# Last projection of an encoder layer: activation sums on VectorE, a written order for the stage, a fourth raw buffer, and the low parts of one product by an accumulating DMA

## The chip, the core and the metric

The kernel runs on one core of a Trainium2 chip. TensorE (PE) multiplies, VectorE (DVE), ScalarE (ACT) and GpSimd (POOL) work elementwise, SyncE (SP) issues most DMAs and GpSimd the others. Every engine takes its instructions in the order in which they stand in the program, and waits on semaphores. Time is device time of one execution in microseconds (us); lower is better.

## The reference

One transformer-like layer on 512 tokens of width 1024, in fp32: a mixer, a cross-attention, a gated feed-forward block, and a last norm. The change touches the end of it alone: the product with `w_down`, the residual sum and the norm.

```python
def swiglu(h, w_gate, w_up, w_down):
    return (jax.nn.silu(h @ w_gate) * (h @ w_up)) @ w_down
...
        x = x + swiglu(rms_norm(x, norm_ffn_g[l]), w_gate_ffn[l], w_up_ffn[l], w_down_ffn[l])
    return rms_norm(x, final_g)
```

The hidden width is 2816, so `w_down` is 2816 x 1024 and the activations are 512 x 2816.

## The kernel before

**How a product is made.** An fp32 factor is cut in two: ScalarE copies it to a rounded high part (`hi`, tiles `wh`, `arh`, `aTh`), VectorE subtracts that from the source to get the low part (`lo`, tiles `wl`, `arl`, `aTl`). Three matmuls (hi x hi, hi x lo, lo x hi) stand for one. `split` does both halves of the cut, and `part` issues the six matmuls (two rows of 128 hidden columns times three) of one token tile with one cut piece of weights.

**The stage.** The hidden columns lie in eleven pairs of 128. Three pairs (`NP = 3`, `c` = 0, 1, 2) are multiplied plainly by `plain` into both column halves of the output. The other eight (`NS = 8`, tile `afb`) go through a scheme of seven block products in place of eight: `a11`, `a12`, `a21`, `a22` are the blocks by parity of the hidden tile and by half of the tokens, `W` is cut alike. Three products take their activations as they lie and four take sums of blocks, formed in place in `afb`; four take differences of weights, two of them formed in place in `wx` (which holds the raw block that several differences need). A product has four chunks of weights (each 128 x 1024 fp32, a half of a raw tile `wr`) and, for each, two token tiles, so eight calls of `part`, 48 matmuls 512 columns wide. The results collect in the PSUM tiles `pa`, `pb`, `pc`, `pd` (`pd` is the second pair of the tiles named `pb` in the trace) and `pe` (named `pf` there); `into` adds a result to the residual `xr` on VectorE, `done` and `last_norm` finish a token tile, and the outputs are stored as they become ready.

**Who did the sums.** `asum` forms the four sums of activations in two halves each, eight instructions on GpSimd (L1212). `wsub` forms the differences of weights on VectorE (L1227). `left` cuts the activations, `prod` the weights (both through `split`, L104 on ScalarE and L105 on VectorE).

**What set the order.** The stage before it (class `Seven`, the gate and up projections) is pinned: instructions recorded with `pin` keep the order in which they are written. The last projection's instructions were not pinned, apart from a few in `fill`: a scheduler placed each of them by its own estimate, between and behind pinned ones. Raw weights go through three buffers (tag `wr`), cut weights through six (tag `wh`/`wl`, `WB = 6`), cut activations through five.

```python
    def asum(o, p, q, op):
        for hs_ in AH:
            nc.gpsimd.tensor_tensor(out=o[:, hs_], in0=p[:, hs_], in1=q[:, hs_], op=op)
```

Of the kernel before, what the change touches and what calls it, by code (L numbers as in the profile page):

```python
# [17 lines left out]
def encoder_kernel(  # L18
# [82 lines left out]
    def split(src, hi, lo, scale=None):

        if scale is None:
            nc.scalar.copy(out=hi, in_=src)  # L104
            nc.vector.tensor_tensor(out=lo, in0=src, in1=hi, op=ALU.subtract)  # L105
# [1057 lines left out]
    def part(dst, a, w, first, last):  # L1163

        n = 0
        for u, v in ((0, 0), (0, 1), (1, 0)):
            for k in range(2):
                nc.tensor.matmul(dst, a[u][:, k, :], w[v][:, k, :], start=first and n == 0, stop=last and n == 5,  # L1168
                                 skip_group_check=True)
# [40 lines left out]
    def asum(o, p, q, op):  # L1210
        for hs_ in AH:
            nc.gpsimd.tensor_tensor(out=o[:, hs_], in0=p[:, hs_], in1=q[:, hs_], op=op)  # L1212
# [5 lines left out]
    def wload(par, half, h, dst=None):  # L1218
        if dst is None:
            return load_raw(wsrc(par, half, h), NS // 2, 512)  # L1220
        nc.sync.dma_start(out=dst, in_=wsrc(par, half, h))
        return dst

    PAIRS = [slice(2 * j, 2 * j + 2) for j in range(NS // 4)]

    def wsub(o, p, q):
        nc.vector.tensor_tensor(out=o, in0=p, in1=q, op=ALU.subtract)  # L1227
        return o

    def wraw(par, half, dst=None):  # L1230

        for h in range(2):
            r = wload(par, half, h, dst and dst[:, AH[h]])
            for sl in PAIRS:
                yield r[:, sl]

    def wform(par, half, f):

        for h in range(2):
            r = wload(par, half, h)  # L1240
            for sl in PAIRS:
                yield f(r[:, sl], wx[:, AH[h]][:, sl])

    def prod(dsts, a, ws, first, last, tail=0):

        pcs = []
        n = NS // 2
        for c, src in enumerate(ws):
            h = wp.tile([P, 2, 512], F32R, name=nm("wh"), tag="wh", bufs=WB)
            l = wp.tile([P, 2, 512], F32R, name=nm("wl"), tag="wl", bufs=WB)  # L1250
            split(src, h, l)
            pcs.append((h, l))

        def go(c, t):
            k = 2 * c % (NS // 2)
            part(dsts[t], [v[:, k:k + 2, TOK[t]] for v in a[2 * c // (NS // 2)]], pcs[c],
                 first and c == 0, last and c == n - 1)

        for c in range(n - tail):
            for t in range(2):  # L1260
                go(c, t)
        for t in range(2):
            for c in range(n - tail, n):
                go(c, t)
# [10 lines left out]
    a11, a12, a21, a22 = blk(0, 0), blk(1, 0), blk(0, 1), blk(1, 1)
    open_a(2)
    for t in range(2, NT):
        plain(bd.dsts[t], 0, 1, t)
    asum(a21, a21, a22, ALU.add)
    l12 = left(a12)  # L1280
    for t in range(NT):
        plain(bd.dsts[t], 0, 2, t)
    open_a(0)
    close(apa)
    ep = pool("ep")
    gfin = ep.tile([P, D], F32, name="gfin")
    nc.gpsimd.dma_start(out=gfin, in_=final_g.partition_broadcast(P))

    xg = {}

    def last_norm(t, half):
        rs = square_half(ep, t, xr[t], half, lead[t])
        if half == lead[t]:
            if t == NT - 1:
                xg[t] = ep.tile([P, 512], F32, name="xg")
                nc.vector.tensor_tensor(out=xg[t], in0=xr[t][:, HALVES[half]], in1=gfin[:, HALVES[half]], op=ALU.mult)
            return
        o = ep.tile([P, D], F32, name=nm("o"), tag="o", bufs=2)
        for h in (lead[t], 1 - lead[t]):
            cs = HALVES[h]  # L1300
            if h == lead[t] and t in xg:
                nc.scalar.activation(out=o[:, cs], in_=xg[t], func=AF.Copy, scale=rs)
            else:
                nc.vector.scalar_tensor_tensor(out=o[:, cs], in0=xr[t][:, cs], scalar=rs, in1=gfin[:, cs],
                                               op0=ALU.mult, op1=ALU.mult)
            nc.sync.dma_start(out=out[t * P:(t + 1) * P, cs], in_=o[:, cs])
# [7 lines left out]
    prod(pb, l12, wraw(1, 0), False, True)  # L1314
    into(pb, 0, 0)
    l11 = left(a11)
    prod(pa, l11, wraw(0, 0, wx), True, True)
    into(pa, 0, 0)
    done(0, 0)
    asum(a11, a21, a11, ALU.subtract)  # L1320
    s1 = left(a21)
    asum(a12, a12, a11, ALU.subtract)
    prod(pc, s1, wform(0, 1, lambda w, x_: wsub(x_, w, x_)), True, True)
    into(pc, 1, 1)
    asum(a21, a22, a11, ALU.subtract)
    s2 = left(a11)
    prod(pa, s2, wform(1, 1, lambda w, x_: wsub(x_, w, x_)), False, True)
    into(pa, 0, 1)
    pe = [acc() for t in range(2)]
    for c in range(NP):  # L1330
        for t in range(NT):
            dst = pc[t] if t < 2 else pe[t - 2]
            plain(dst, 1, c, t, first=t >= 2 and c == 0, last=c == NP - 1)
    into(pe, 1, 1)
    s4 = left(a12)
    prod(pc, s4, wraw(1, 1), False, True)
    into(pc, 0, 1)
    done(0, 1)
    s3 = left(a21)
    prod(pa, s3, wform(0, 0, lambda w, x_: wsub(w, x_, w)), False, True)  # L1340
    into(pa, 1, 1)
    done(1, 1)
    into(pa, 1, 0)
    l22 = left(a22)
    prod(pd, l22, wform(1, 0, lambda w, x_: wsub(w, w, x_)), False, True, tail=2)
    for t in range(2):
        nc.vector.tensor_tensor(out=xr[2 + t][:, HALVES[0]], in0=pd[t], in1=xr[2 + t][:, HALVES[0]], op=ALU.add)
# [41 lines left out]
```

## Time and profile before

| | us |
|---|---|
| median of 3 runs | 970.9 (970.65 to 973.08) |
| the profiled execution | 969.74 |
| its span, first to last instruction | 968.0 |
| PE busy | 945.1 |
| DVE busy | 705.4 |
| ACT busy | 480.1 |
| POOL busy | 259.1 |
| granted TensorE clock, mean | 0.992 |

Every line of the profile belongs to the one profiled execution. A row of the timeline has the start, the duration, the engine, the source line (L1168 is line 1168), the operation, tiles written and read, and how many instructions were merged into the row; a bracket at its end is the idle time before it and what ended that. The last projection begins at about 841.7 us, with the first matmul of `part`.

### The profile page before, as it was taken

What the parts mean: (1) busy time and instruction counts of PE and PEld (TensorE: products, weight loads), DVE (VectorE), ACT (ScalarE), POOL (GpSimd) and SP (SyncE); (2) the same over time, 40 slices, a digit from 0 to 9 for tenths busy, and PEclk for the clock granted to TensorE, in tenths of its full rate; (3) what the DMA queues carried; (4) which work ended last, traced back from release to release, by engine and by line L of the source; (5) the groups of instructions that cost most, each with busy time, mean ns of one, the idle gap of its engine ahead of it and who ended that gap; (6) DMA issues with size and microseconds to landing.
All of it is one profiled execution on the core that took longest, in us unless ns stands there. A gap on an engine that the chain in (4) does not pass through costs nothing. (4 is left out here: it accounts for less than half of the span.)

```text
span 968.0 us, 14495 instructions
## 1 busy us (share of the span) xinstructions
PE 945.1 (98%) x5894; PEld 849.1 (88%) x5894; DVE 705.4 (73%) x859; ACT 480.1 (50%) x742; POOL 259.1 (27%) x215
## 2 busy tenths in 40 slices
PE   7999999999999999999999999999999999998996
PEld 7988888888999999988988887899999999987785
DVE  6677887668965667566835445699888888799975
ACT  6474665435544545437635334554555455553632
POOL 1221122263411544321000000144454544264000
PEclk8999999999999999999999999999999999999998
DMA  8421221320432333381553211204333324452532
GB/s 292 144 88 44 87 78 54 120 88 22 131 109 88 110 89 109 101 290 44 175 173 131 87 44 49 79 5 131 99 120 102 118 88 130 153 196 87 177 106 87
DMA packets 83682, 107.12 MB, mean 111 GB/s; under 512 B 2096, under 2 KB 63584, under 8 KB 83616
## 3 DMA queue, kind: packets, MB, share of 16 engines
q1 hardware_dynamic: 82368, 101.74, 32.2%
q0 software_dynamic: 1248, 4.46, 1.3%
q8 instruction: 46, 0.75, 0.3%
q14 instruction: 20, 0.16, 0.1%
HBM read 104.10 MB, written 2.10 MB: 110 GB/s over the span
## 5 line engine op out<-in xcount | busy, mean ns | idle before, releaser
L105 DVE TENSOR_TENSOR wl<-wr,wh 128x1024 fp32r<-128x1024 f32 x100 | 124.9, 1259 | 63.0 <-ACT wh L104 37.3
L272 DVE TENSOR_TENSOR wl<-wr,wh 128x1024 fp32r<-128x1024 f32 x93 | 136.1, 1474 | 29.2 <-ACT wh L267 29.2
L104 ACT CAST wh<-wr 128x1024 fp32r<-128x1024 f32 x100 | 103.6, 1049 | 88.6 <-PE pq L142 20.9
L267 ACT CAST wh<-wr 128x1024 fp32r<-128x1024 f32 x93 | 97.7, 1052 | 26.1 <-DVE wr L257 26.1
L174 POOL TENSOR_TENSOR rs<-ve,mhalf 128x1 f32<-128x1 f32 x22 | 14.5, 661 | 314.6 <-DVE ve L172 249.7
L250 POOL TENSOR_TENSOR s<-wr 128x512 f32<-128x512 f32 x31 | 40.7, 1313 | 114.6 <-DVE w L272 110.4
L286 ACT COPY u<-pf 128x256 f32<-128x256 f32 x62 | 23.2, 374 | 93.2 <-DVE g L1098 33.8
L251 POOL TENSOR_TENSOR wr<-wr 128x512 f32<-128x512 f32 x31 | 64.6, 2084 | 2.4
L806 POOL TENSOR_TENSOR merged<-merged,sg 128x512 f32<-128x512 f32 x16 | 27.5, 1724 | 79.9 <-DVE sg L805 79.9
L582 POOL TENSOR_SCALAR_AFFINE_SELECT ab<-ab 128x128 f32<-128x128 f32 x32 | 23.8, 776 | 80.1 <-ACT ab L579 80.1
L280 PE MATMUL pf<-h3th,wh 128*128 128x256 f32 x240 | 37.1, 277 | 0.4 <-ACT m L286 0.4
L280 PE MATMUL pf<-h3tl,wh 128*128 128x256 f32 x240 | 37.0, 276 | 0.0
L280 PE MATMUL pf<-h3th,wl 128*128 128x256 f32 x240 | 37.0, 276 | 0.0
L286 ACT COPY m<-pf 128x256 f32<-128x256 f32 x31 | 11.6, 373 | 47.3 <-PE pf L280 45.1
L280 PEld LDWEIGHTS pf<-h3th,wh 128*128 128x128 f32 x240 | 31.7, 188 | 0.7 <-ACT m L286 0.6
L280 PEld LDWEIGHTS pf<-h3tl,wh 128*128 128x128 f32 x240 | 31.7, 188 | 0.0
L280 PEld LDWEIGHTS pf<-h3th,wl 128*128 128x128 f32 x240 | 31.7, 188 | 0.0
L257 DVE TENSOR_TENSOR wr<-wr 128x512 f32<-128x512 f32 x31 | 30.2, 975 | 1.1
L183 ACT ACTIVATE jk<-xr 128x512 f32<-128x512 f32 x24 | 15.1, 630 | 30.5 <-DVE xr L886 13.1
L1125 POOL TENSOR_TENSOR afb<-afb,g 128x256 f32<-128x256 f32 (+1 forms) x16 | 19.4, 1210 | 36.9 <-DVE afb L1098 36.9
L1212 POOL TENSOR_TENSOR afb<-afb 128x1024 f32<-128x1024 f32 x8 | 27.1, 3403 | 7.6 <-DVE arl L105 7.5
L280 PE MATMUL pf<-h3h,wh 128*128 128x256 f32 x160 | 25.6, 282 | 2.1 <-DVE g L1098 2.1
(381 smaller groups left out, 2638.3 us busy)
## 6 DMA issues: line engine op xcount, KB each, us to landing
wr<-in_w_in_dram SPq DMA_DIRECT2D x26, 1024.0 KB, 5.3
wr<-in_w_down_ffn_dram SPq DMA_DIRECT2D x14, 1024.0 KB, 5.1
wr<-in_w_gate_ffn_dram SPq DMA_DIRECT2D x11, 1024.0 KB, 5.4
wr<-in_w_up_ffn_dram SPq DMA_DIRECT2D x11, 1024.0 KB, 5.4
wb<-in_w_branch_dram SPq DMA_DIRECT2D x12, 512.0 KB, 3.3
wr<-in_w_out_dram SPq DMA_DIRECT2D x4, 1024.0 KB, 8.9
wr<-in_w_k_xa_dram SPq DMA_DIRECT2D x4, 1024.0 KB, 8.7
wr<-in_w_v_xa_dram SPq DMA_DIRECT2D x4, 1024.0 KB, 5.1
```

The source lines that it names most:

```text
L104: nc.scalar.copy(out=hi, in_=src)
L105: nc.vector.tensor_tensor(out=lo, in0=src, in1=hi, op=ALU.subtract)
L250: pin(nc.gpsimd.tensor_tensor(out=self.s1, in0=r[:, 0:4, P:256], in1=r[:, 4:8, P:256], op=ALU.add))
L251: pin(nc.gpsimd.tensor_tensor(out=r[:, 0:4, P:256], in0=r[:, 0:4, 0:P], in1=r[:, 0:4, P:256], op=ALU.subtract))
L257: pin(nc.vector.tensor_tensor(out=r[:, 4:8, 0:P], in0=r[:, 4:8, 0:P], in1=r[:, 0:4, 0:P], op=ALU.subtract))
L267: pin(nc.scalar.copy(out=t[0], in_=src))
L272: pin(nc.vector.tensor_tensor(out=l, in0=src, in1=h, op=ALU.subtract))
L280: pin(nc.tensor.matmul(dst[:, 0:256], w[:, k, :], v[:, k, :], start=first and n == 0, stop=last and n == 11, skip_group_check=True))
L286: pin(nc.scalar.copy(out=m, in_=self.a[:, 0:256]))
L582: nc.gpsimd.affine_select(out=dg, in_=dg, compare_op=ALU.is_gt, fill=0.0, base=0, channel_multiplier=1, pattern=[[-1, P]])
L806: pin(nc.gpsimd.tensor_tensor(out=merged[:, d, :], in0=merged[:, d, :], in1=sg, op=ALU.add))
L1212: nc.gpsimd.tensor_tensor(out=o[:, hs_], in0=p[:, hs_], in1=q[:, hs_], op=op)
```

## The change

Four things are changed, all in the last projection:

1. The eight sums of activations go from GpSimd to VectorE (`dsub`, L1207). GpSimd keeps the four small powers of the last norm and DMA issues.
2. All of the stage is pinned in a written order. The work is a list of steps, one per chunk of weights (two token tiles, 12 matmuls). Around the matmuls of step i - 5 the list issues the cut of step i, the sums and differences of step i + 2, and the loads of step i + 4; a low part is issued on VectorE one step behind its high part. The plain products of column half 1 are split: two pairs stand between the third product and the fourth, the last pair behind the fifth product. The norm's first squares of token tiles 0 and 1 move from behind the second product to behind the fourth.
3. A fourth buffer for raw weights: every fourth raw tile lies in a pool of its own.
4. In the third product (into `pc`, sum `a21 + a22`) the four low parts of the weights are made without VectorE: ScalarE writes minus the high part into `wl` (L1201), and a DMA issued by GpSimd adds the source to it (L1202). Source and destination are both in SBUF, 512 KB each.

The two cut tiles of plain pair 2 and of pair 0 lie in tiles of their own, and cut activations have four buffers instead of five. The order of the matmuls within a chunk, and the split of the last product by token tile (`tail=2`), stay.

```diff
-                nc.tensor.matmul(dst, a[u][:, k, :], w[v][:, k, :], start=first and n == 0, stop=last and n == 5,
-                                 skip_group_check=True)
+                pin(nc.tensor.matmul(dst, a[u][:, k, :], w[v][:, k, :], start=first and n == 0, stop=last and n == 5,
+                                     skip_group_check=True))
...
-    def asum(o, p, q, op):
-        for hs_ in AH:
-            nc.gpsimd.tensor_tensor(out=o[:, hs_], in0=p[:, hs_], in1=q[:, hs_], op=op)
+    los = []
+
+    def cut_pinned(src, hi, lo, added=False):
+        pin(nc.scalar.copy(out=hi, in_=src))
+        if added:
+            pin(nc.scalar.activation(out=lo, in_=hi, func=AF.Copy, scale=-1.0))
+            pin(nc.gpsimd.dma_start(out=lo, in_=src, accum_op=ALU.add))
+        else:
+            los.append(lambda: dsub(lo, src, hi))
+
+    def dsub(o, p, q, op=ALU.subtract):
+        pin(nc.vector.tensor_tensor(out=o, in0=p, in1=q, op=op))
...
+    RAWS = 4
+    raws = {"n": 0}
+
+    def raw_tile():
+        raws["n"] += 1
+        if raws["n"] % RAWS == 0:
+            return ad1.tile([P, NH, 512], F32, name=nm("wr"), tag="wr", bufs=1)
+        return wp.tile([P, NH, 512], F32, name=nm("wr"), tag="wr", bufs=3)
...
+        def sums(c):
+            h = c // 2
+            if c % 2 == 0 and asum is not None:
+                dsub(act[:, AH[h]], *(v[:, AH[h]] for v in asum[:2]), *asum[2:])
+            sl = slice(2 * (c % 2), 2 * (c % 2) + 2)
+            x_ = wx[:, AH[h]][:, sl]
+            src[c] = x_ if wraw is None else got[h][:, sl]
+            if wform is not None:
+                src[c] = wform(src[c], x_)
...
+    product(PB, a12, None, (1, 0), None, False, lambda: into(pb, 0, 0))
+    product(PA, a11, None, None, None, True, lambda: into(pa, 0, 0))
+    product(PC, a21, (a21, a22, ALU.add), (0, 1), tform(True, False), True, lambda: into(pc, 1, 1), added=True)
+    for q in zip(half1(0), half1(1)):
+        for v in q:
+            step(*v)
+    product(PA, a11, (a21, a11), (1, 1), tform(True, False), False, after6)
+    product(PC, a12, (a12, a11), (1, 1), None, False, lambda: None)
+    q = half1(2)
+    step(*q[0])
+    step(*q[1], post=lambda: (after3(), into(hold["e"], 1, 1)))
+    product(PA, a21, (a22, a11), (0, 0), tform(False, True), False, after7)
+    product(PD, a22, None, (1, 0), tform(False, False), False, after4, tail=2)
+
+    HIS, SUM, MORE = 5, 2, 4
+    late = {}
+    for i in range(-MORE, len(steps) + HIS):
+        for k, d in ((0, MORE), (1, SUM), (2, 0)):
+            if 0 <= i + d < len(steps):
+                steps[i + d][k]()
+        late[i], los[:] = los[:], []
+        for f in late.pop(i - 1, ()):
+            f()
+        if i >= HIS:
+            steps[i - HIS][3]()
+            steps[i - HIS][4]()
```

The order of instructions on the engines shows what moves. GpSimd, in the fourth-last pair of the gate and up projections (L1125 is the product of gate and up, L250 and L251 are sums of gate or up weights):

```order
 L1125 TENSOR_TENSOR afb<-afb,g_7411 128x256
 L1125 TENSOR_TENSOR afb<-afb,g_7411 128x512
-L1212 TENSOR_TENSOR afb<-afb 128x4x256
 L250 TENSOR_TENSOR s_7689<-wr_7550 128x512
 L251 TENSOR_TENSOR wr_7550<-wr_7550 128x4x128
```

One half of a sum of activations had been placed there, well ahead of the last projection; it is gone. GpSimd, from the last product of gate and up to the end:

```order
 L1125 TENSOR_TENSOR afb<-afb,g_8389 128x256
 L1125 TENSOR_TENSOR afb<-afb,g_8389 128x512
-L1212 TENSOR_TENSOR afb<-afb 128x4x256
-L1287 DMA gfin<-in_final_g_dram 128x1024
-L1212 TENSOR_TENSOR afb<-afb 128x4x256 x6
...
+L1202 DMA wl_8751<-wx 128x1024
+L1202 DMA wl_8774<-wx 128x1024
+L1202 DMA wl_8795<-wx 128x1024
+L1202 DMA wl_8812<-wx 128x1024
+L1360 DMA gfin<-in_final_g_dram 128x1024
```

The seven other halves are gone too; four accumulating DMAs stand in their place, and the load of the last gain `gfin` now follows them. VectorE after the change, from the adds of the first product's result (`pb`, L1241) through the differences and cuts that the second and third product need (`wx` rows are differences of weights, `afb` rows sums of activations):

```order
L1241 TENSOR_TENSOR xr_3935<-pb_8509,xr_3935 128x512
L1241 TENSOR_TENSOR xr_3936<-pb_8510,xr_3936 128x512
L1207 TENSOR_TENSOR wx<-wr_8664,wx 128x1024
L1207 TENSOR_TENSOR arl_8707<-afb,arh_8706 128x1024
L1207 TENSOR_TENSOR wl_8710<-wx,wh_8709 128x1024
L1207 TENSOR_TENSOR afb<-afb 128x4x256
L1207 TENSOR_TENSOR wx<-wr_8702,wx 128x1024
L1207 TENSOR_TENSOR wl_8727<-wx,wh_8726 128x1024
L1207 TENSOR_TENSOR wx<-wr_8702,wx 128x1024
L1207 TENSOR_TENSOR arl_8748<-afb,arh_8747 128x1024
```

And VectorE before, at the same place:

```order
L1227 TENSOR_TENSOR wx<-wr_8829,wx 128x1024
L105 TENSOR_TENSOR arl_8824<-afb,arh_8823 128x1024
L1227 TENSOR_TENSOR wx<-wr_8829,wx 128x1024
L105 TENSOR_TENSOR wl_8758<-wx,wh_8757 128x1024
L1227 TENSOR_TENSOR wx<-wr_8841,wx 128x1024
L1269 TENSOR_TENSOR xr_3935<-pb_8509,xr_3935 128x512
L105 TENSOR_TENSOR wl_8833<-wx,wh_8832 128x1024
L1269 TENSOR_TENSOR xr_3936<-pb_8510,xr_3936 128x512
```

Before, the adds of `pb` stood among the differences for the third product, four `wl` rows of which follow; now they stand ahead of these, the sums stand among them, and the third product has no `wl` row here. The end of VectorE's row, before (L1347 adds the last product, L188 and L172 make the norm's factor, L1304 writes the output `o`):

```order
L1347 TENSOR_TENSOR xr_3937<-pb_8511,xr_3937 128x512
L188 TENSOR_TENSOR st_9361<-ss_9268,ss_9359 128x1
L172 TENSOR_SCALAR ve_9363<-st_9361 128x1
L1304 SCALAR_TENSOR_TENSOR o_9367<-xr_3937,rs_9365,gfin 128x512 x2
L1347 TENSOR_TENSOR xr_3938<-pb_8512,xr_3938 128x512
L188 TENSOR_TENSOR st_9376<-ss_9271,ss_9374 128x1
```

And after:

```order
L1402 TENSOR_TENSOR xr_3937<-pb_8511,xr_3937 128x512
L188 TENSOR_TENSOR st_9355<-ss_9306,ss_9353 128x1
L172 TENSOR_SCALAR ve_9357<-st_9355 128x1
L1402 TENSOR_TENSOR xr_3938<-pb_8512,xr_3938 128x512
L1377 SCALAR_TENSOR_TENSOR o_9361<-xr_3937,rs_9359,gfin 128x512 x2
L188 TENSOR_TENSOR st_9382<-ss_9309,ss_9380 128x1
```

The add of the last token tile has moved ahead of the two output instructions of the tile before it.

More of the change, by code (lines that the diff above doesn't have):

```diff
@@ L1216, in wsrc, with wload, step, ring @@
         return w[:, AH[h]]
[L1218 to L1264, printed above, removed]
+    RAWS = 4
[5 more added lines that the diff above has]
+        return wp.tile([P, NH, 512], F32, name=nm("wr"), tag="wr", bufs=3)
+    def wload(par, half, h):
+        r = raw_tile()
+        pin(nc.sync.dma_start(out=r, in_=wsrc(par, half, h)))
+        return r
+    steps = []
+    def step(prep, mul, post=lambda: None, load=lambda: None, sums=lambda: None):
+        steps.append((load, sums, prep, mul, post))
+    def ring(src, added=False):
+        h = wp.tile([P, 2, 512], F32R, name=nm("wh"), tag="wh", bufs=WB)
+        l = wp.tile([P, 2, 512], F32R, name=nm("wl"), tag="wl", bufs=WB)
+        cut_pinned(src, h, l, added)
+        return h, l
     def into(dsts, i, half):
@@ L1273, in done @@
             last["f"](2 * i + t, half)
[L1275 to L1306, printed above, removed]
@@ L1308, in encoder_kernel, with product, load, prep @@
-    lead = (0, 0, 1, 1)
-    last["f"] = last_norm
+    def product(dsts, act, asum, wraw, wform, first, post, added=False, tail=0):
+        got, arr = {}, {}
+        def load(c):
+            if c % 2 == 0 and wraw is not None:
+                got[c // 2] = wload(*wraw, c // 2)
+        src = {}
+        def sums(c):
[7 more added lines that the diff above has]
+                src[c] = wform(src[c], x_)
+        def prep(c):
+            for h in range(2):
+                if c == (0 if tail else 2 * h):
+                    arr[h] = tuple(ad1.tile([P, NH, T // 2], F32R, name=nm(f"ar{s}"), tag=f"ar{s}", bufs=4)
+                                   for s in "hl")
+                    cut_pinned(act[:, AH[h]], *arr[h])
+            arr["w", c] = ring(src[c], added)
+        def go(c, t):
+            k = 2 * (c % 2)
+            part(dsts()[t], [v[:, k:k + 2, TOK[t]] for v in arr[c // 2]], arr["w", c], first and c == 0, c == 3)
+        def mul(c):
+            if c < 4 - tail:
+                for t in range(2):
+                    go(c, t)
+            elif c == 3:
+                for t in range(2):
+                    for k in range(4 - tail, 4):
+                        go(k, t)
+                    if t == 0:
+                        post(0)
+        if asum is None and wraw == (1, 0) and not tail:
+            load0, load = load, lambda c: (load0(c), c == 0 and load_x())
+        for c in range(4):
+            step(lambda c=c: prep(c), lambda c=c: mul(c),
+                 (lambda: post(1) if tail else post()) if c == 3 else lambda: None, lambda c=c: load(c),
+                 lambda c=c: sums(c))
@@ L1310, in encoder_kernel @@
+    step(cut2, lambda: plain0(0, (2, 3)))
+    step(prep2, lambda: plain0(1, (2, 3)))
+    step(lambda: None, lambda: plain0(2, (0, 1)))
+    step(lambda: None, lambda: plain0(2, (2, 3)))
     pa = [bank(nm("pa")) for t in range(2)]
@@ L1312, in encoder_kernel @@
     pb, pd = bd.dsts[:2], bd.dsts[2:]
[L1314 to L1343, printed above, removed]
@@ new lines, in encoder_kernel, with after6, after3, after7 @@
+    lead = (0, 0, 1, 1)
+    def after6():
+        into(pa, 0, 1)
+        last["ep"] = open_ep()
+        done(0, 0)
+    def after3():
+        into(pc, 0, 1)
+    def after7():
+        into(pa, 1, 1)
+        done(0, 1)
+        done(1, 1)
+        into(pa, 1, 0)
+    def after4(t):
+        o = xr[2 + t][:, HALVES[0]]
+        nc.vector.tensor_tensor(out=o, in0=pd[t], in1=o, op=ALU.add)
+        last["f"](2 + t, 0)
+    product(PB, a12, None, (1, 0), None, False, lambda: into(pb, 0, 0))
+    product(PA, a11, None, None, None, True, lambda: into(pa, 0, 0))
```

88 lines of the change are left out of this document (70 added, 18 removed).

## The prediction

> **What bounds the kernel now.** I read the page's head first, then TensorE's waits, then the busy time of the last projection's stretches, then its timeline around each wait.
>
> ```profile
> span 968.0 us, 14495 instructions
> PE 945.1 (98%) x5894; PEld 849.1 (88%) x5894; DVE 705.4 (73%) x859; ACT 480.1 (50%) x742; POOL 259.1 (27%) x215
> ...
> PE pa L1168 <- DVE wl L105: 3.9, 2, 2.7
> ...
> PE pf L280 <- DVE g L1098: 2.1, 3, 1.7
> ```
>
> TensorE is busy 98% of the span, so a change that takes no matmul away can only win back TensorE's waits, what the clock loses behind them, and the tail. The two rows of waits (total, times, longest) say that both kinds that matter here end with VectorE.
>
> ```profile
> 850.00:884.00 34.00, 31.28 (x138) 25.63 (x137) 33.40 (x17) 13.87 (x14) 24.65 (x8) 1.00 0.46 162
> 884.00:906.00 22.00, 20.81 (x85) 16.66 (x85) 22.00 (x23) 13.65 (x17) 0.00 (x0) 0.92 0.36 127
> ```
>
> These are stretches of the last projection; the columns after the length are the busy time of PE, weight loads, DVE, ACT and POOL, then the granted clock. VectorE has work in 55.4 of 56 us, and in the first stretch GpSimd is busy 24.65 beside it. What that costs VectorE:
>
> ```profile
> L105 DVE TENSOR_TENSOR wl<-wx,wh 128x1024 fp32r<-128x1024 f32 x12 | 22.5, 1890 | 0.6 <-ACT wh L104 0.6
> L105 DVE TENSOR_TENSOR arl<-afb,arh 128x1024 fp32r<-128x1024 f32 x10 | 14.1, 1436 | 0.0
> L1227 DVE TENSOR_TENSOR wx<-wr,wx 128x1024 f32<-128x1024 f32 x8 | 11.9, 1491 | 0.0
> L105 DVE TENSOR_TENSOR aTl<-af,aTh 128x1024 fp32r<-128x1024 f32 x2 | 4.6, 2318 | 0.0
> ...
> 898.00 1.22 DVE L105 TENSOR_TENSOR arl<-afb,arh 128x1024 fp32r<-128x1024 f32 x1
> 899.13 1.22 DVE L105 TENSOR_TENSOR wl<-wx,wh 128x1024 fp32r<-128x1024 f32 x1
> ...
> 859.87 17.81 POOL L1212 TENSOR_TENSOR afb<-afb 128x1024 f32<-128x1024 f32 x5 [6.30 <-DVE arl L105]
> ```
>
> With GpSimd idle a VectorE instruction of 128x1024 takes 1.22 and the next starts 1.13 behind it. The groups (848 to 907 us) have means of 1.44 to 2.32. The excess is 12 x 0.67 + 10 x 0.22 + 8 x 0.27 + 2 x 1.10 = 14.6 us, and it lies where GpSimd does its sums. The waits it leads to:
>
> ```profile
> 879.46 0.62 PE L1168 MATMUL pa<-wh,arl 128*128 128x512 f32 x2
> 879.92 0.61 PE L1168 MATMUL pa<-wh,arh 128*128 128x512 f32 x2
> 883.26 0.73 PE L1168 MATMUL pa<-wl,arh 128*128 128x512 f32 x2 [2.72 <-DVE wl L105]
> ...
> 885.42 1.05 PE L1168 MATMUL pa<-wl,arh 128*128 128x512 f32 x2
> 886.27 1.05 PE L1168 MATMUL pa<-wh,arl 128*128 128x512 f32 x2
> ...
> 888.17 0.62 PE L1168 MATMUL pc<-wh,arl 128*128 128x512 f32 x2
> ...
> 898.15 1.07 PE L1168 MATMUL pa<-wh,arh 128*128 128x512 f32 x4
> 900.41 0.73 PE L1168 MATMUL pa<-wl,arh 128*128 128x512 f32 x2 [1.19 <-DVE wl L105]
> ```
>
> A pair of matmuls normally follows the last after 0.453 (879.46 to 879.92). From 879.92 to 888.17 there are eight steps, 3.63 at that pace; they took 8.25. So this wait costs 4.6: 2.9 of waiting and 1.7 of slow pairs (0.85 apart) behind it. The second: 898.15 to 900.41 should be 0.91 and is 2.26; 1.35, and 0.1 for the slower pair behind it.
>
> A third lies earlier, in the gate and up projections:
>
> ```profile
> 754.96 0.62 PE L280 MATMUL pf<-h3th,w 128*128 128x256 f32 x4
> 755.75 0.74 PE L280 MATMUL pf<-h3h,wh 128*128 128x256 f32 x4 [0.17 <-DVE g L1098]
> ...
> 774.87 0.62 PE L280 MATMUL pf<-h3th,w 128*128 128x256 f32 x4
> 777.22 0.74 PE L280 MATMUL pf<-h3h,wh 128*128 128x256 f32 x4 [1.74 <-DVE g L1098]
> ...
> 770.16 2.73 POOL L1212 TENSOR_TENSOR afb<-afb 128x1024 f32<-128x1024 f32 x1
> ...
> 770.56 2.89 DVE L272 TENSOR_TENSOR w<-s,w 128x512 fp32r<-128x512 f32 x1
> ```
>
> The first two rows are one period of this stage, the next two the period in which the scheduler had put a half sum. At 770.16 GpSimd adds for 2.73 us, VectorE's 128x512 subtraction at 770.56 takes 2.89 beside it, and TensorE's step is 2.35 where it was 0.79 the period before: 1.6 lost.
>
> **The change, part by part.**
>
> *Sums to VectorE.* Eight halves leave GpSimd; VectorE gets 8 x 1.13 = 9.0 us and loses the excess of 14.6. The early half sum disappears from the gate and up stage and nothing replaces it: 1.6 us back there, with no cost, as its place on VectorE is now in the last projection.
>
> *Low parts by DMA.* VectorE loses four `wl`, 4 x 1.13 = 4.5. So VectorE is relieved of 14.6 + 4.5 - 9.0 = 10.1 us in the stretch in which it had no idle time and was late by 2.9 + 1.35 us. The relief covers the lateness 2.4 times. ScalarE gets four instructions of 128x1024 more:
>
> ```profile
> L104 ACT CAST wh<-wx 128x1024 fp32r<-128x1024 f32 x12 | 12.5, 1051 | 25.3 <-DVE wx L1227 21.2 <-DMA wx<-in_w_down_ffn_dram 4.1
> ```
>
> 4 x 1.05 = 4.2 us on an engine that stood 25.3 us idle ahead of this very group; nothing on the path.
>
> *Written order.* It adds waits on VectorE: the adds of a result stand at fixed places and wait for TensorE. Let P be the end of the first product (about 871 us). Behind its second add (done at P + 0.65) queue `wx`, `arl`, `wl`: 3 x 1.13, P + 4.1. A chunk is 12 matmuls, 2.72; TensorE wants that `wl` (second product, chunk 2) at P + 2 x 2.72 + 0.45 = P + 5.9. Then sum, `wx`, `wl`: P + 7.5, wanted at P + 8.6. These are the tightest places, 1.1 us to spare; later products have five chunks of lead. Cost 0, up to 1.5 if rows run long.
>
> *Fourth raw buffer.* Loads start four chunks (10.9 us) ahead of their first use and land in 5.1 (row below): hidden; if that cover went, the first use would be late by what the load queue adds.
>
> *The accumulating DMA.* The trace has none. Nearest rows: plain loads by SyncE and GpSimd, the same queue's issues, VectorE beside those.
>
> ```profile
> wr<-in_w_down_ffn_dram SPq DMA_DIRECT2D x13, 1024.0 KB, 5.1
> wr<-in_w_down_ffn_dram SPq DMA_DIRECT2D x2, 512.0 KB, 3.5
> gfin<-in_final_g_dram POOLq DMA_DIRECT2D x1, 512.0 KB, 4.4
> ...
> wr<-in_w_out_dram SPq DMA_DIRECT2D x4, 1024.0 KB, 8.9
> ...
> 408.59 2.19 POOL L908 DMA_DIRECT2D xr<-in_x_dram x4
> ...
> 407.41 3.46 DVE L105 TENSOR_TENSOR wl<-wr,wh 128x1024 fp32r<-128x1024 f32 x2
> ```
>
> 512 KB more cost 1.6 us; a plain 512 KB from GpSimd's queue lands in 4.4, the low end. The high end is 8.9, loads queued behind others. An accumulate reads source and destination, so I take twice the bytes: 4.4 + 1.6 = 6.0. The cover: chunk 0's source exists early; its minus is written by P - 0.6 and TensorE wants the low part at P + 4 x 2.72 + 0.45 = P + 11.3. Chunk 1 waits for the second `wx` row (P + 1.8), then two ScalarE instructions, P + 4; wanted P + 14. Chunk 2: four VectorE rows later, P + 6.4, then P + 8.6; wanted P + 16.8. Chunk 3: P + 11; wanted P + 19.5. The least cover is 8.2, so 6.0 costs nothing and 8.9 costs 0.7. `gfin`, now behind them, is wanted 50 us later. What waits behind an accumulate on GpSimd is only the next one.
>
> *Tail.*
>
> ```profile
> 959.02 0.61 PE L1168 MATMUL pb<-wh,arl 128*128 128x512 f32 x2
> ...
> 959.51 1.41 DVE L1304 SCALAR_TENSOR_TENSOR o<-xr,rs,gfin 128x512 f32<-128x512 f32 x2 [0.66 <-POOL rs L174]
> 960.84 0.69 DVE L1347 TENSOR_TENSOR xr<-pb,xr 128x512 f32<-128x512 f32 x1
> 962.37 0.16 DVE L188 TENSOR_TENSOR st<-ss,ss 128x1 f32<-128x1 f32 x1 [0.85 <-ACT jk L183]
> ```
>
> TensorE ends at E = 959.63, but the last add starts at 960.84 because two `o` rows stand ahead. After the change it starts at E + 0.05, then the two `o` rows (1.33) run while ScalarE squares; `st` follows at E + 0.05 + 0.6 + 1.33 = E + 2.0 where it was E + 2.74: 0.75 gained.
>
> At the start of the stage TensorE's pinned order brings one group of the gate and up stage forward by two groups, behind a copy and an add of 0.4 each: 0 to 0.5 lost, I take 0.2.
>
> Sum: 4.6 + 1.45 + 1.6 + 0.75 - 0.2 = 8.2. The profiled execution was 969.74 (span 968.0 and 1.7 around it): 961.5. It stands 1.2 below the median of the runs, 970.9, from which the same 8.2 gives 962.7.
>
> [...]
>
> **The rivals.**
>
> *Slow accumulates (ends on the other side).* If one takes s of DMA time and they follow each other, the fourth lands at P - 0.6 + 2.8 + 4s (2.8 being the 4.4 less 1.6) against P + 19.5: late from s = 4.3, by 4s - 17.3, and 1.7 of slow clock behind it. At s = 6 that is 8.4 and takes the whole gain, 971.1; at s = 6.7 it is slower by 0.3%; at s = 8, five times the plain 1.6, 979. For it: no row shows an accumulate. Against: the bytes explain 3.2. Chance 0.14, of which slower 0.09.
>
> *Accumulates a little late* (landing 9 to 11, s of 4.4 to 5.3): 1 to 5 lost with the clock, 964 to 968. Chance 0.13.
>
> *VectorE late again,* at the places with 1.1 to spare or at an add: one or two waits of 1 to 2 us with slow pairs, 964.5 to 968. For it: 68 rows of 1.13 and 12 adds of 0.6, 84 us, in the 95 us of the stage. Against: the excess is gone and the waits that remain sit ahead of work with chunks of lead. Chance 0.10.
>
> *GpSimd's issues starve.* [...] Against: the four issues at 408.59 take 2.19 in all, beside VectorE subtractions in a row. Chance 0.03. [...]
>
> *It doesn't do what it says:* the waits come from the number of VectorE's rows, not from GpSimd beside them, and return elsewhere: 970 to 971.5. Against: 2.89 for a 128x512. Chance 0.05.
>
> **How the numbers follow.** The forecast, 962.7, has 0.55 (its own range 960.7 to 964.4: the tail and the start by 0.5 each way, and 1.2 between the profiled execution and the median). With it the two partial cases (0.23) reach to 968.5, which leaves out 0.2 together with the slow accumulates' upper part; the lower end is 960.5. A change of 0.3%, 2.9 us, is about what a measurement can tell here. Faster by more than that (under 968.0): 0.55 + 0.12 + 0.09 + 0.02 = 0.78. Slower: 0.09 + 0.03 = 0.12. The rest, 0.10, is no difference.
>
> **What would show it.** Right: no GpSimd sum and no VectorE 128x1024 above 1.25 us; TensorE's waits for `wl` gone between 850 and 906 and the step at 774.87 like its neighbours; granted clock 1.00 there; the accumulates landing within 8 us; `st` 2.0 behind TensorE's end. Wrong: a wait of TensorE in `pc` ended by a DMA (slow accumulates); GpSimd's DMA rows stretched over 1 us (starving); waits of `pa` ended by VectorE at the second product's chunks 2 and 3 (late again).

## The result, and the profile after

| | before | after |
|---|---|---|
| median | 971.26 (970.65 to 973.08, 4 runs) | 965.56 (965.46 to 965.95, 4 runs) |
| the profiled execution | 969.74 | 965.52 |
| its span | 968.0 | 963.6 |

After is 0.9939 of before, 95% interval 0.9922 to 0.9956: 5.7 us by the medians, 4.2 between the two profiled executions. 962.7 had been forecast, with 8.2 of gain.

I read the page's head of the changed kernel first, then the list of what TensorE waited for.

```profile
span 963.6 us, 14493 instructions
...
PE 946.7 (98%) x5894; PEld 853.2 (89%) x5894; DVE 692.9 (72%) x863; ACT 485.4 (50%) x746; POOL 235.1 (24%) x211
```

```profile
PE pf L280 <- ACT m L286: 0.4, 1, 0.4
PE pbr L798 <- ACT wh L786: 0.4, 1, 0.4
PE pt L204 <- DVE h L424: 0.3, 1, 0.3
PE pf L280 <- DVE g L1098: 0.2, 1, 0.2
```

The row of `pa` with 3.9 us is gone, and no row of L1168 has taken its place. `pf` behind `g` fell from 2.1 to 0.2. And yet TensorE's busy time went up, from 945.1 to 946.7, with the same 5894 matmuls. That is the first sign that the matmuls themselves went slower somewhere.

The last projection's two stretches (columns as before: length, PE, weight loads, DVE, ACT, POOL, clock):

```profile
850.00:884.00 34.00, 34.00 (x151) 28.16 (x151) 25.42 (x24) 20.92 (x21) 2.28 (x3) 1.00 0.73 237
884.00:906.00 22.00, 22.00 (x98) 18.23 (x98) 20.64 (x21) 13.99 (x17) 1.84 (x3) 1.00 0.95 288
```

TensorE has no gap, the clock is 1.00, and VectorE, which had work in 55.4 of 56 us, has it in 46.1. Its rows, and the accumulating DMAs:

```profile
L1207 DVE TENSOR_TENSOR wl<-wx,wh 128x1024 fp32r<-128x1024 f32 x8 | 9.8, 1219 | 0.0
L1207 DVE TENSOR_TENSOR afb<-afb 128x1024 f32<-128x1024 f32 x8 | 9.7, 1217 | 0.0
...
wl<-wx POOLq DMA_DIRECT2D x4, 512.0 KB, 5.5
...
874.35 0.93 POOL L1202 DMA_DIRECT2D wl<-wx  x1 [25.23 <-PE pb L1168]
```

The mean of a `wl` row fell from 1.89 to 1.22, the eight sums take 1.22 each, and an accumulate landed 5.5 after its issue. The tail:

```profile
955.46 0.61 PE L1168 MATMUL pb<-wh,arl 128*128 128x512 f32 x2
956.11 0.69 DVE L1402 TENSOR_TENSOR xr<-pb,xr 128x512 f32<-128x512 f32 x1 [0.83 <-PE pb L1168]
956.72 1.41 DVE L1377 SCALAR_TENSOR_TENSOR o<-xr,rs,gfin 128x512 f32<-128x512 f32 x2
...
958.04 0.15 DVE L188 TENSOR_TENSOR st<-ss,ss 128x1 f32<-128x1 f32 x1
```

The last add starts 0.04 behind TensorE's end (956.07), the `o` rows run beside ScalarE's square, and `st` follows 1.97 behind the end.

What took the rest of the gain lies ahead of the changed stage. The gate and up projections, where TensorE has the same instructions in the same order, start 0.4 earlier (648.50 for 648.90) and end 2.6 later: the first matmul of L1168 is at 844.29, where it was at 841.72. TensorE's timeline there, after:

```profile
657.80 0.62 PE L280 MATMUL pf<-h3tl,w 128*128 128x256 f32 x4
658.25 0.62 PE L280 MATMUL pf<-h3th,w 128*128 128x256 f32 x4
659.04 0.74 PE L280 MATMUL pf<-h3h,wh 128*128 128x256 f32 x4 [0.17 <-DVE g L1098]
659.61 0.63 PE L280 MATMUL pf<-h3l,wh 128*128 128x256 f32 x4
660.08 0.63 PE L280 MATMUL pf<-h3h,wl 128*128 128x256 f32 x4
```

Four matmuls of 256 columns followed one another every 0.453 us up to 658.25; behind a wait of 0.17 they follow every 0.471, and do so for 185 us, up to the end of the stage. Before had the same wait at the same instruction and went on at 0.453:

```profile
658.66 0.62 PE L280 MATMUL pf<-h3th,w 128*128 128x256 f32 x4
659.44 0.74 PE L280 MATMUL pf<-h3h,wh 128*128 128x256 f32 x4 [0.17 <-DVE g L1098]
660.02 0.62 PE L280 MATMUL pf<-h3l,wh 128*128 128x256 f32 x4
660.47 0.62 PE L280 MATMUL pf<-h3h,wl 128*128 128x256 f32 x4
```

A window of 40 us shows it, first before, then after (the number in brackets behind PE's busy time counts matmuls):

```profile
680.00:720.00 40.00, 40.00 (x352) 39.75 (x351) 33.38 (x40) 21.13 (x36) 18.48 (x12) 1.00 0.36 107
```

```profile
680.00:720.00 40.00, 40.00 (x342) 40.00 (x341) 33.10 (x39) 20.68 (x36) 18.48 (x12) 1.00 0.35 106
```

342 matmuls where there were 352, at the same granted clock of 1.00, with weight loads running all of the time.

### The profile page after: what moved, and what is told of

The parts are those of the page before. It is cut to its first block, busy times and chain, and to the rows that moved or that the text cites. A ratio compares the mean times of both kernels' runs of the same rounds, so it can differ in the third digit from the quotient of the medians.

```text
span 963.6 us, 14493 instructions
## 1 busy us (share of the span) xinstructions
PE 946.7 (98%) x5894; PEld 853.2 (89%) x5894; DVE 692.9 (72%) x863; ACT 485.4 (50%) x746; POOL 235.1 (24%) x211
## 5 line engine op out<-in xcount | busy, mean ns | idle before, releaser
L250 POOL TENSOR_TENSOR s<-wr 128x512 f32<-128x512 f32 x31 | 40.7, 1314 | 115.1 <-DVE w L272 111.0
L251 POOL TENSOR_TENSOR wr<-wr 128x512 f32<-128x512 f32 x31 | 64.6, 2084 | 2.4
L280 PE MATMUL pf<-h3th,wh 128*128 128x256 f32 x240 | 38.1, 281 | 0.4 <-ACT m L286 0.4
L280 PE MATMUL pf<-h3th,wl 128*128 128x256 f32 x240 | 38.0, 281 | 0.0
L280 PE MATMUL pf<-h3tl,wh 128*128 128x256 f32 x240 | 38.0, 281 | 0.0
L280 PEld LDWEIGHTS pf<-h3th,wh 128*128 128x128 f32 x240 | 32.5, 189 | 0.7 <-ACT m L286 0.6
L280 PEld LDWEIGHTS pf<-h3th,wl 128*128 128x128 f32 x240 | 32.7, 190 | 0.0
L280 PEld LDWEIGHTS pf<-h3tl,wh 128*128 128x128 f32 x240 | 32.4, 189 | 0.0
L257 DVE TENSOR_TENSOR wr<-wr 128x512 f32<-128x512 f32 x31 | 30.2, 976 | 1.1
L1125 POOL TENSOR_TENSOR afb<-afb,g 128x256 f32<-128x256 f32 (+1 forms) x16 | 18.5, 1153 | 39.7 <-DVE afb L1098 38.1
L1207 DVE TENSOR_TENSOR wl<-wr,wh 128x1024 fp32r<-128x1024 f32 x20 | 23.9, 1218 | 2.8 <-ACT wh L1199 2.8
```

The costliest lines, as they stand in the source:

```text
L250: pin(nc.gpsimd.tensor_tensor(out=self.s1, in0=r[:, 0:4, P:256], in1=r[:, 4:8, P:256], op=ALU.add))
L251: pin(nc.gpsimd.tensor_tensor(out=r[:, 0:4, P:256], in0=r[:, 0:4, 0:P], in1=r[:, 0:4, P:256], op=ALU.subtract))
L257: pin(nc.vector.tensor_tensor(out=r[:, 4:8, 0:P], in0=r[:, 4:8, 0:P], in1=r[:, 0:4, 0:P], op=ALU.subtract))
L280: pin(nc.tensor.matmul(dst[:, 0:256], w[:, k, :], v[:, k, :], start=first and n == 0, stop=last and n == 11, skip_group_check=True))
L1207: pin(nc.vector.tensor_tensor(out=o, in0=p, in1=q, op=op))
```

## The experiments

Two questions: what gave the gain in the last projection, and whether the slow pace belongs to the change. Three numbers of each profile answer them: the length of the gate and up stage (first group of L280 to first matmul of L1168), that of the last projection (from there to TensorE's last end), and what is left from there to the end of the span. The profiled execution's time stands beside them, then the median of all runs and the ratio to before with its interval (the medians of before beside the experiments were 969.6 to 970.0).

| kernel | profiled | stage | last projection | rest | median | ratio |
|---|---|---|---|---|---|---|
| before | 969.74 | 192.8 | 117.9 | 8.4 | 971.26 | |
| after | 965.52 | 195.8 | 111.8 | 7.5 | 965.56 | 0.9939 (0.9922 to 0.9956) |
| e1 before, early sum late | 969.86 | 190.6 | 120.1 | 8.4 | 969.68 | 1.0006 (0.9991 to 1.0022) |
| e2 after, one kick | 962.78 | 192.6 | 111.8 | 7.5 | 962.32 | 0.9922 (0.9906 to 0.9939) |
| e3 after, sums on GpSimd | 973.24 | 193.5 | 120.2 | 8.3 | 970.23 | 1.0018 (1.0004 to 1.0032) |
| e4 after, no accumulates | 962.59 | 190.6 | 111.9 | 9.8 | 962.63 | 0.9936 (0.9918 to 0.9953) |
| f1 after again | 966.09 | 195.8 | 111.8 | 7.5 | 963.50 | 0.9931 (0.9913 to 0.9950) |
| f2 after, extra matmuls | 967.18 | 197.9 | 111.8 | 7.5 | 961.61 | 0.9928 (0.9903 to 0.9954) |
| f3 e4 with another tail | 960.40 | 190.6 | 111.9 | 8.3 | 962.90 | 0.9924 (0.9904 to 0.9943) |
| f4 before, sums on VectorE | 964.54 | 193.6 | 111.8 | 9.2 | 963.75 | 0.9939 (0.9917 to 0.9960) |
| g1 after, three raw buffers | 963.08 | 190.6 | 114.1 | 7.6 | 962.05 | 0.9921 (0.9902 to 0.9941) |
| g2 after, many kicks | 968.53 | 198.9 | 111.8 | 7.5 | 968.39 | 0.9979 (0.9966 to 0.9993) |
| g3 after, twelve accumulates | 969.66 | 190.6 | 117.9 | 11.1 | 969.82 | 1.0008 (0.9991 to 1.0025) |
| g4 f4 with the tail's order | 962.20 | 191.5 | 111.8 | 8.5 | 962.14 | 0.9923 (0.9907 to 0.9939) |

**e1: the kernel before, its sums in written order on GpSimd.**

```diff
-            nc.gpsimd.tensor_tensor(out=o[:, hs_], in0=p[:, hs_], in1=q[:, hs_], op=op)
+            pin(nc.gpsimd.tensor_tensor(out=o[:, hs_], in0=p[:, hs_], in1=q[:, hs_], op=op))
```

> The kernel before, with the half sum of 770.16 kept out of the gate and up stage (GpSimd's sums in written order); every other engine's order stays. My sum: the step at 774.87 becomes 0.79 like its neighbours, 1.6 us less, unless the sum, now 75 us later, makes VectorE later in the last projection. Theory A (TensorE has two steady paces in this stage, 0.453 and 0.471 us for four 256-column matmuls, and what happens at a wait decides which): the pace may turn to 0.471 here, and then the stage is 3 us longer instead. Theory B (the pace belongs to the program, 0.453 in every variant of before, 0.471 in every variant of after): 0.453 and 1.6 us faster.

The time did not move (0.9991 to 1.0022). The stage came down from 192.8 to 190.6, so the early half sum had cost 2.2 there. The last projection gave it back, 120.1 for 117.9: with all eight sums in it, the wait for `wl` grew from 2.72 to 4.92.

```profile
883.40 1.22 PE L1168 MATMUL pa<-wl,arh 128*128 128x512 f32 x2 [4.92 <-DVE wl L105]
```

The half that I gave as a condition ("unless the sum, now 75 us later, makes VectorE later in the last projection") came true. The pace was 0.453 throughout, so this run says nothing of theory A.

**e3: the kernel after, its sums back on GpSimd.**

```diff
-                dsub(act[:, AH[h]], *(v[:, AH[h]] for v in asum[:2]), *asum[2:])
+                gsub(act[:, AH[h]], *(v[:, AH[h]] for v in asum[:2]), *asum[2:])
```

`gsub` is `dsub` on GpSimd, pinned.

> The kernel after with its eight half sums on GpSimd, everything else as it is. My sum: VectorE's 128x1024 rows beside them get longer again (by 0.67 to 1.1 us each, some 14 us in all), less the 9.0 us of sums that VectorE no longer does; with the four low parts away by DMA (4.5 us) TensorE's waits of 2.7 and 1.2 come back in part: 967 to 970. Rival (the waits came from the unwritten order, not from GpSimd): no wait, 965.6. Rival (GpSimd's sums hold up its own accumulating DMAs): a wait in the third product, over 970.

All of the last projection's gain is gone, 120.2 for 111.8, in the written order, with four raw buffers and the accumulates; TensorE's instructions stand in the same order as in the kernel after, one by one. So the rival of the unwritten order is out, and no wait stands in the third product, as the other rival had it. The time, 970.2, is just above my 967 to 970. The waits did not come back as 2.7 and 1.2: one wait of 6.04 took their place, behind a single VectorE instruction.

```profile
884.03 5.07 POOL L1210 TENSOR_TENSOR afb<-afb 128x1024 f32<-128x1024 f32 x2
...
889.35 9.64 POOL L1210 TENSOR_TENSOR afb<-afb 128x1024 f32<-128x1024 f32 x4
...
884.55 15.53 DVE L1207 TENSOR_TENSOR aTl<-af,aTh 128x1024 fp32r<-128x1024 f32 x1
...
901.27 1.22 PE L1168 MATMUL pf<-wl,aTh 128*128 128x512 f32 x2 [6.04 <-DVE wl L1207]
```

Six sums in a row on GpSimd, from 884.03 to 898.99, and a VectorE subtraction (1.22 us where GpSimd is idle) that starts in the first of them takes 15.53 and ends 1.1 behind the last. Its row is about as long as the six sums, which take 14.96 from the first's start to the last's end. In the kernel before, a VectorE instruction had been about as long as one sum: beside the five sums of the row at 859.87 (17.81 in all) five of its instructions took 2.7 to 3.4 each. That VectorE stands while GpSimd adds is my reading of these lengths; no row shows what makes it stand, and why one instruction of e3 spans six sums is open.

**f4: the kernel before, its sums on VectorE.**

```diff
-            nc.gpsimd.tensor_tensor(out=o[:, hs_], in0=p[:, hs_], in1=q[:, hs_], op=op)
+            nc.vector.tensor_tensor(out=o[:, hs_], in0=p[:, hs_], in1=q[:, hs_], op=op)
```

> The kernel before with its eight half sums on VectorE and nothing else changed (the order stays the scheduler's; two of the sums stand in or at the end of the gate and up stage, GpSimd being free there). My sum: VectorE is rid of 14.6 us of excess and takes 9.0; the step at 774.87 loses its 1.6; of the waits of 2.7 and 1.2 with their slow pairs (6.05) most go: 5 to 7.5 us faster than before. Rival (the written order is needed, since the scheduler puts the sums ahead of what TensorE waits for): waits of 2 to 4 stay, 0 to 3 us faster.

One word of the diff gives all of the last projection's gain, 111.8, with the scheduler's order, three raw buffers and no accumulate. The rival is refuted: no wait of L1168 is left. The word is the only difference of the source, not of the program: with the sums on VectorE, the scheduler also ordered TensorE's matmuls from the second product to the fourth, and rows of VectorE and ScalarE, in another way. So f4 shows that the other parts are not needed, and e3, where TensorE's order is that of the kernel after, that the engine of the sums matters. Its profile also shows the pace turn, at a wait in the middle of the stage:

```profile
773.28 0.62 PE L280 MATMUL pf<-h3tl,w 128*128 128x256 f32 x4
773.73 0.62 PE L280 MATMUL pf<-h3th,w 128*128 128x256 f32 x4
775.21 0.74 PE L280 MATMUL pf<-h3h,wh 128*128 128x256 f32 x4 [0.86 <-DVE g L1098]
775.78 0.63 PE L280 MATMUL pf<-h3l,wh 128*128 128x256 f32 x4
776.25 0.63 PE L280 MATMUL pf<-h3h,wl 128*128 128x256 f32 x4
```

0.45 a group up to there, 0.47 from there to the end of the stage.

**e4 and f3: the kernel after without accumulates, and that with the last add ahead of the rows of `o`.**

```diff
-    product(PC, a21, (a21, a22, ALU.add), (0, 1), tform(True, False), True, lambda: into(pc, 1, 1), added=True)
+    product(PC, a21, (a21, a22, ALU.add), (0, 1), tform(True, False), True, lambda: into(pc, 1, 1))
```

> The kernel after with the third product's four low parts on VectorE instead of by accumulating DMA. My sum: VectorE was relieved by 14.6 of excess and takes 9.0 of sums; with 4.5 more it is still 1.1 us better off than before in a stretch in which it was late by 2.9: a wait of TensorE of 1 to 2 us, with slow pairs behind it 2 to 4: 967 to 969. Rival (written order and a chunk's lead of the low parts suffice): no wait, 965.6.

> The kernel after with the third product's low parts on VectorE (no accumulating DMA) and with the last add written ahead of the two rows of o of the tile before, on VectorE. From e4_after_no_accumulate, whose last add started at 953.81, 2.75 behind TensorE's end, where the kernel after has 0.04: the end comes 2.0 to 2.3 us earlier than there, 960.3 at the pace of 0.453. Also, the time outside the span was 1.7 without the accumulating DMAs and 1.9 to 2.1 with them; here 1.7. If the low parts by DMA were worth something: TensorE waits in the third product again, over 962.

My sum failed in e4, the rival held: the last projection is 111.9 without a wait, so the low parts by DMA are worth nothing where the sums stand on VectorE. What differed was the tail, 9.8 for 7.5: the scheduler, left to order it, put the rows of `o` ahead of the last add. The text of the tail is the kernel after's; the change does not pin that add, and e3 and g3 (rests of 8.3 and 11.1) have it behind the rows of `o` too. f3 wrote that order down and got 1.5 of it back (8.3; I had said 2.0 to 2.3: the add was pinned behind the row `ve`, 0.7 behind TensorE's end). f3's quickest execution, 960.40, is the shortest time of all; its others reach 965.37.

**g4: f4 with the order of the tail.**

```diff
-    for t in range(2):
-        nc.vector.tensor_tensor(out=xr[2 + t][:, HALVES[0]], in0=pd[t], in1=xr[2 + t][:, HALVES[0]], op=ALU.add)
-        last["f"](2 + t, 0)
+    nc.vector.tensor_tensor(out=xr[2][:, HALVES[0]], in0=pd[0], in1=xr[2][:, HALVES[0]], op=ALU.add)
+    last["f"](2, 0, lambda: add(1))
+    last["f"](3, 0)
```

The add of tile 3 is recorded, pinned, behind tile 2's row `ve`, and tile 2's rows of `o`, pinned too, behind that add.

> f4_before_sums_vector with the last add written ahead of the two rows of o of the tile before. There TensorE ended at 953.58 and the span at 962.8, 9.2 later; the kernel after has 7.5. So 1.7 us less than f4 at the same pace: 960.3 at 0.453 throughout, and a median about 962. If the written order, the fourth buffer and the accumulates of the kernel after were worth something beside the sums and the tail, this one stays above it by that much.

962.14, with 961.8 to 963.02 in six runs: as good as the kernel after, with the sums and the tail's order alone. `st` stood 1.97 behind TensorE's end, 2.74 in f4, so the order gives the 0.75 that I had priced. That the rest is 8.5 and not 7.5 is the last store of `o`, which landed 3.2 us behind its issue here and 2.3 in the kernel after; why is open.

**g1: three raw buffers.**

```diff
-    RAWS = 4
+    RAWS = 1000
```

> The kernel after with three raw buffers instead of four in the last projection. My sum priced the fourth at nothing, loads starting 10.9 us ahead and landing in 5 to 6. With three a load waits for the buffer freed one tile later, some 5 us less lead: no wait of TensorE, the last projection 111.8 us long as in the kernel after, the time within the spread of the paces (960 to 966). Rival (the fourth buffer is what lets VectorE run ahead): waits of TensorE or of VectorE on a load, 2 us or more in the last projection.

My sum failed. The rival had the size, but not the mechanism: the last projection is 2.3 longer, and TensorE's waits are for accumulates, not for loads, as in my rival "accumulates a little late" of the prediction:

```profile
887.70 0.73 PE L1168 MATMUL pc<-wl,arh 128*128 128x512 f32 x2 [1.46 <-DMA wl<-wx]
...
890.94 0.74 PE L1168 MATMUL pc<-wl,arh 128*128 128x512 f32 x2 [0.20 <-DMA wl<-wx]
...
wl<-wx POOLq DMA_DIRECT2D x4, 512.0 KB, 7.5
```

The accumulates were issued at the same points of the stage (30.2 us in, after: 30.1) and landed in 7.5 instead of 5.5. SyncE's rows of the loads in that stretch, with three buffers and then with four (after):

```profile
878.30 10.90 SPq L1224 DMA_DIRECT2D wr<-in_w_down_ffn_dram  x4
```

```profile
876.37 17.26 SPq L1224 DMA_DIRECT2D wr<-in_w_down_ffn_dram  x4
```

Four loads are issued within 10.9 us, where four buffers had spread four over 17.3. That the loads are what delayed the accumulates was not tried by itself. So the fourth buffer is worth 2.3 beside the accumulates, and f4 shows that it is worth nothing without them.

**g3: accumulates in three products.** (`added=True` for the fourth and fifth product too.)

> The kernel after with the low parts of three products by accumulating DMA, twelve in place of four. If an accumulate lands in 5.5 us as the four did, TensorE sees none of it: the last projection 111.8 us long. VectorE is 9 us freer there. The time outside the span (1.7 without, 1.9 to 2.1 with four) grows if it belongs to the accumulates, to about 2.5. Rival (slow accumulates): waits of TensorE in the fourth and fifth product.

The rival came nearer than my sum. Eight accumulates landed in 7.9 and four in 9.8, and the last projection is 117.9. The longest waits were not for the accumulates but for VectorE, which had itself waited for a raw tile:

```profile
DVE wr L1207 <- DMA wr<-in_w_down_ffn_dram: 14.7, 1, 14.7
...
926.70 0.73 PE L1168 MATMUL pf<-wl,aTh 128*128 128x512 f32 x2 [2.21 <-DVE wl L1207]
```

So the low cost of four accumulates does not carry over to twelve. What delays them, the loads, each other, or both, was not tried by itself. The time outside the span, which I had put down to them, is 1.9 to 2.1 in six kernels with four (after, e2, e3, f1, f2, g1) and 1.7 in the six kernels without, but also 1.7 in g2 with four and 1.7 to 1.8 here with twelve. Accumulates alone do not make it, and what it is stays open.

**e2, f1, f2, g2: whose is the pace?** e2 writes one low part of 128x1024 twice on VectorE (fifth of 20 items), g2 one of 128x512 in 15 items; f2 issues the first matmul of 19 items twice; f1 changes nothing.

```diff
                 q.lo(b)
+                if z == 20 and k == 4:
+                    q.lo(b)
```

> The kernel after with one low part of the gate and up stage written twice on VectorE (the same values), in the fifth of 20 items, so that TensorE waits there once for about 1 us. Theory A: the pace behind that wait can be another than before it; if it turns to 0.453 the rest of the stage (some 150 us at 0.471) takes up to 5 us less, less the wait: 961 to 963. Theory B: 0.471 stays, and it is slower by the wait, 966 to 967.

> The kernel after once more, unchanged, to see whether its pace in the gate and up stage (0.471 us for four matmuls in its first profile, from 659.61 to the stage's end) is its own. Theory A (two steady paces, and what happens at single waits decides which): other executions have 0.453 over part or all of the stage; then the time is 1 to 4 us lower than 965.6 beside the same before, about 960 to 962 where before is 969.6. Theory B (0.471 belongs to this program): 4 us less than before again.

> The kernel after with the first matmul of 19 items of the gate and up stage issued twice (the same product, overwritten by the second): 19 x 0.113 = 2.2 us more work, and the count of matmuls between two waits becomes odd. Theory A: if the pace hangs on how weight loads and matmuls stand to each other behind a wait, an odd count changes how often each of the two paces comes; I expect single items at 0.471 and others at 0.453 within one profile. If it hangs on something else: the paces come as in the kernel after, and the time is 2.2 more.

> The kernel after with one more low part of 128x512 (0.69 us on VectorE, the same values) in 15 items of the gate and up stage, so that TensorE waits there some 15 times. Theory A (a wait can turn the pace either way): within one profile the pace changes at several of these waits, from 0.471 to 0.453 and back, and never between two waits. Rival (once at 0.471 it stays so to the end of the stage): no change from 0.471 to 0.453. The waits cost 3 to 10 us in all.

Theory B fell with e2: its pace was 0.453 from 659.90 on, before the kick as behind it, and with a wait of 2.15 too many it took 962.3. So it told nothing of what a wait does. f1 is the plain answer on the time: the unchanged kernel took 961.13, 962.92, 963.04, 963.97, 964.13 and 966.09. The profile taken of it was the 966.09, with the stage at 0.471 from 660.18 to its end, and 195.8 long. Kernels that kept 0.453 there (e1, e4, f3, g1, g3) have 190.6; over the whole stage the slower pace costs 5.2 us. Four of these five are variants of the kernel after, and f4, the kernel before with one word changed, turned to 0.471. So the pace is not bound to the change. That one and the same program has now the one pace and now the other is inferred from its times alone: f1's spread over 5.0, and both profiles taken of the kernel after are at 0.471. f2 missed my expectation of single slow items: two of its runs took 967.0 and 967.2 and four 960.8 to 961.8, and the profile, one of the two, is at 0.471 throughout the stage. An odd count does not decide it.

g2 shows both turns in one profile:

```profile
696.93 0.62 PE L280 MATMUL pf<-h3th,w 128*128 128x256 f32 x4
698.26 0.74 PE L280 MATMUL pf<-h3h,wh 128*128 128x256 f32 x4 [0.72 <-DVE g L1100]
698.84 0.64 PE L280 MATMUL pf<-h3l,wh 128*128 128x256 f32 x4
699.31 0.63 PE L280 MATMUL pf<-h3h,wl 128*128 128x256 f32 x4
...
717.21 0.63 PE L280 MATMUL pf<-h3tl,w 128*128 128x256 f32 x4
717.68 0.63 PE L280 MATMUL pf<-h3th,w 128*128 128x256 f32 x4
718.68 0.74 PE L280 MATMUL pf<-h3h,wh 128*128 128x256 f32 x4 [0.37 <-DVE g L1100]
719.26 0.62 PE L280 MATMUL pf<-h3l,wh 128*128 128x256 f32 x4
719.72 0.62 PE L280 MATMUL pf<-h3h,wl 128*128 128x256 f32 x4
```

Behind the wait of 0.72 the groups go from 0.45 to 0.47, and behind the wait of 0.37, 20 us later, back to 0.45. Five further waits of about 1.1 left it at 0.45. Inside the stage it changed only at such places, in all of the profiles; some of these waits are so short that the row has no bracket, only a step longer by 0.1 to 0.3 (e3 at 736.73, f1 at 659.60). The ten runs of g2 lie within 2.2 us (967.1 to 969.34).

At the stage's ends it also changed without a wait. In every profile, a few groups of 256 columns follow behind the first pairs of 512 columns of the last projection, and they go at 0.471, also where the stage had been at 0.453 up to there. Before, with no idle time in these rows:

```profile
844.00 0.61 PE L1168 MATMUL pb<-wh,a0l 128*128 128x512 f32 x2
844.45 0.63 PE L280 MATMUL pf<-h3th,wh 128*128 128x256 f32 x4
844.92 0.63 PE L280 MATMUL pf<-h3tl,wh 128*128 128x256 f32 x4
```

So theory A holds as far as this: there are two steady paces for one and the same stream, and within the stage the one gives way to the other at waits. A wait is not the only place at which it turns, as the first rows behind the stage show. In after, f1 and f2, all at 0.471, TensorE has no wait from 660 us to the stage's end, which fits that the pace stays there. Why a given wait turns it or not is open: before and after have the same wait of 0.17, f4 and g4 the same of 0.86, and in each pair only one turned.

## Why the prediction was right, and where it was off

The range held the time and the forecast's side was right. The main case's own range, 960.7 to 964.4, did not hold 965.56: the time fell into the part that had been added for late accumulates and a late VectorE, neither of which came. That the range held these four runs is luck in this respect; the six of f1 have their median, 963.50, inside the main case. By its steps:

- *Sums to VectorE, the two waits, 4.6 + 1.45.* Right: the last projection went from 117.9 to 111.8, 6.1. e3 (sums back: 120.2) and f4 (111.8 without the other parts) put it on this part.
- *The early half sum, 1.6.* This is the step that failed: "1.6 us back there, with no cost". The stage became 3.0 longer (192.8 to 195.8) instead. The term itself was about right, 2.2 by e1; what I had not seen was that TensorE's matmuls can go at another pace. At 0.453 the stage is 190.6, at 0.471 it is 195.8. All four runs of the first comparison lie between 965.46 and 965.95, near f1's slowest (966.09) and 4.4 above its quickest. Their paces, apart from the profiled one's, were not recorded.
- *Tail, 0.75.* Right, 0.86 (8.37 to 7.51); `st` 1.97 behind TensorE's end for 2.0 forecast. It is the scheduler's placing of an add that the change does not pin, as e3, e4 and g3 show.
- *Low parts by DMA.* Landing 5.5 for 6.0, no wait: right on its cost. The relief of 4.5 for VectorE was worth nothing (e4).
- *Written order.* Cost 0, as forecast, and no wait at the tight places. It was worth nothing either beside the tail (f4).
- *Fourth raw buffer, 0.* Off: 2.3 beside the accumulates (g1). I had asked whether the loads come in time, not whether the accumulates land as early with three buffers.
- *Start of the stage, -0.2.* Not seen apart from the pace.

In numbers, between the two profiled executions: 0.4 ahead at the start of the gate and up stage, 3.0 lost in it, 6.1 and 0.86 won, 4.4 in the span; 0.2 were lost outside the span.

Of the rivals, "accumulates a little late" came true only when one of the change's own parts was taken away (g1), there with a landing of 7.5; the 9 to 11 that the prediction puts beside its s of 4.4 to 5.3 do not follow from its own 2.8 + s, which gives 7.2 to 8.1. GpSimd's issues took 0.93 at most; nothing starved. The slow pairs that I charged to a wait by its row returned, behind 2.21 (g3), 4.92 (e1) and 6.04 (e3).

## What to carry to other kernels

An engine's mean duration that is well above its shortest row can be a price that another engine charges (here 1.89 for a `wl` row of VectorE with sums on GpSimd, 1.22 without): look for who runs beside it, and try moving that work before adding buffers or orders. Here one word, the engine of eight sums, did all that the change did in its stage. When a stage whose instructions did not change takes another time, count its matmuls per window at equal clock and run the kernel again before you seek a reason in the change.

## What the runs showed of the hardware

**Two paces of TensorE.** A stream of 256-column fp32 matmuls, each with its own weight load, ran at 0.453 or at 0.471 us for four, 4% apart, with the granted clock at 1.00 in both. Pairs of 512 columns in the last projection followed one another every 0.453 in all profiles where the clock was 1.00, except for one or two behind a wait (0.57 and 0.47 in g1, from 887.70). In the slower pace the weight loads are busy 40.00 of 40 us (after, 680 to 720), in the faster 39.75 (before, the same window).

**The clock behind a wait.** A wait of 2.15 (e2) left the clock at 1.00; one of 2.21 (g3) was followed by half the clock:

```profile
700.50:703.90 3.40, 3.40 (x32) 3.40 (x31) 3.09 (x4) 2.23 (x6) 0.00 (x0) 1.00 0.34 100
```

```profile
927.60:930.90 3.30, 3.30 (x10) 2.56 (x9) 3.30 (x4) 2.85 (x3) 0.00 (x0) 0.50 0.94 304
```

How long the half clock lasts: in before, behind the wait of 2.72, the trace's clock record has 0.50 for 3.41 us. For the others I estimate it from the mean clocks of windows: about 3.4 in g3 (0.96, 0.50 and 0.99 in windows of 1.0, 3.3 and 2.1 us), and 6.8 behind 4.92 in e1 (0.89 and 0.94 in two windows of 20 us) and behind 6.04 in e3 (0.84 and 0.99 in two of 20). Before's wait of 1.74, at 777.22, left the clock at 1.00, like the 2.15 of e2. What tells 2.15 from 2.21 no run shows.
